# A two-layer decoder trunk on one core: the second product of the feed-forward blocks by Strassen's seven products

## The chip, the cores and the metric

One core of one Trainium2 chip runs the whole program. Time is device microseconds (us) of one execution, taken from three runs without a profile. Beside them one execution was recorded by the hardware profiler. Its span is counted from the first to the last instruction.

The engines named below are PE (matrix products; PEld are its weight loads), DVE (vector), ACT (scalar), POOL (GpSimd), and SP, which issues DMAs. PSUM is the memory in which PE sums products, in eight banks of 128x512 fp32. SBUF is the on-chip memory, HBM the memory outside.

## The reference, cut to what is computed

Two layers, each with four sub-layers (here called phases): `ff1`, a token mixer `mix`, attention into a memory `mem`, and `ff2`. Both feed-forward phases are the same function, so that it runs four times.

```python
D_MODEL, SEQ, DEPTH, D_FF = 1024, 512, 2, 2816
def swiglu(h, w1, w3, w2):
    return (jax.nn.silu(h @ w1) * (h @ w3)) @ w2
for l in range(DEPTH):
    h = rmsnorm(x, ff1_pre_g[l])
    x = x + 0.5 * rmsnorm(swiglu(h, ff1_w1[l], ff1_w3[l], ff1_w2[l]), ff1_post_g[l])
    ... # x = x + rmsnorm(token_mixer(rmsnorm(x))); x = x + rmsnorm(cross_attention(rmsnorm(x), mem))
    h = rmsnorm(x, ff2_pre_g[l])
    x = x + 0.5 * rmsnorm(swiglu(h, ff2_w1[l], ff2_w3[l], ff2_w2[l]), ff2_post_g[l])
```

All is in float32.

## The kernel before

**Products.** A float32 product is made of three products of PE's reduced float32 type: each operand is split into a high part and a remainder, and high by high, high by low and low by high are summed in PSUM (`mm3`, `mm`). Splitting takes ACT for the high part and DVE for the remainder (`split` for activations, `Weights.parts` for weights).

**Weights.** `plan` lists the weight blocks of the whole program in the order of their use. `Weights.pump` issues one SP DMA of 512 KB for each into one of three buffers `raw`. ACT writes the high part and DVE the remainder into one of four buffers `wh`. The remainder frees `raw`; `ahead`, 2 or 4, says how many blocks may be split before their use.

**A feed-forward phase** (`ffn`). The hidden features are 22 blocks of 128. For each, `project` multiplies the normed tokens (`hh`, `hlo`) by a block of w1 and one of w3: 24 matmuls of 128x512 each. `gate` makes the activation from the two banks by a tanh on ACT and two operations on DVE, and splits it into a tile `g`. The first four blocks go through `first_blocks`: all four for tokens 0 to 255 first, then for 256 to 511, so that PE can begin while the last tokens are still normed. This is called the gate stage here.

**The second product** (`token_out`) follows: out = g · w2, by token tiles m = 0 to 3 of 128 tokens, two halves of 512 output features, and 22 blocks of contraction, of which a w2 block holds two. That is 4 x 2 x 22 x 3 = 528 matmuls of 128x512, in four banks for each half of the features. The last four w2 blocks of the second half run token tile by token tile, and after each tile comes its `chain`: a sum of squares on ACT, the product with the gain, small operations on DVE, a power on POOL (`rstd`), and the update of x. Where a phase follows, `pre_norm` norms the token tile, PE transposes it (`tr`), and ACT and DVE split it into `hh` and `hlo`; in the last phase SP writes x to HBM.

**Order.** Each engine runs its instructions in the order in which the program lists them. This order is laid down at build time by a planner (`Clock`), which runs the parts of the code as tasks against estimated times. At run time nothing changes it: an instruction whose input is late holds up all behind it on its engine.

Of the kernel before, what the change touches and what calls it, by code (L numbers as in the profile page):

```python
# [10 lines left out]
F32 = mybir.dt.float32  # L11
F32R = mybir.dt.float32r
# [7 lines left out]
NT = S // 128  # L20
NF = FF // 128
EPS = 1e-6
# [27 lines left out]
def pack(inp):  # L50
# [14 lines left out]
    for f in ("ff1", "ff2"):  # L65
        o[f + "_w1"] = stationary(a[f + "_w1"], NF)
        o[f + "_w3"] = stationary(a[f + "_w3"], NF)
        o[f + "_w2"] = moving(a[f + "_w2"])
# [38 lines left out]

def plan(d):
    items = []

    def add(key, ap, split=True):
        items.append((key, ap, split))

    for l in range(DEPTH):
        for ph in PHASES:
            if ph in ("ff1", "ff2"):
                for i in range(NF):
# [186 lines left out]
class Block:  # L304
    __slots__ = ("raw", "hl", "cols", "ready")


class Weights:


    def __init__(self, b, items, raws, hls):
        self.b, self.items, self.raws, self.hls = b, items, Slots(raws), Slots(hls)
        self.blocks = {}
        self.n_dma = self.n_prep = self.n_use = self.ahead = 0
        self.dma = 0.0

    def pump(self, most=3):
        b, ck = self.b, self.b.ck
        while True:
            moved = False  # L320
            if most and self.n_dma < len(self.items) and self.raws.free:
                most -= 1
                key, ap, split = self.items[self.n_dma]
                k = Block()
                k.cols = ap.shape[-1]
                when, _, k.raw = self.raws.pop()
                k.hl = None
                b.nc.sync.dma_start(k.raw[:, :k.cols], ap)
# [19 lines left out]
    def parts(self, k):  # L348
        b, n = self.b, k.cols
        raw, hi, lo = k.raw[:, :n], k.hl[:, 0, :n], k.hl[:, 1, :n]  # L350
        yield b.act(hi, raw, AF.Copy)
        r = b.tt(lo, raw, hi.bitcast(F32), OP.subtract)
        self.raws.put(r, k.raw)
# [31 lines left out]
class Builder:  # L385
# [70 lines left out]
    def build(self):  # L456
        tc, nc, d, ck = self.tc, self.nc, self.d, self.ck
        with tc.tile_pool(name="fixed", bufs=1) as fixed, \
                tc.tile_pool(name="upper", bufs=1, side="right") as upper, \
                tc.tile_pool(name="small", bufs=4, side="right") as small, \  # L460
                tc.tile_pool(name="psum", bufs=1, space=bass.MemoryType.PSUM) as psum, \
                tc.manual_schedule():
# [4 lines left out]
            raws = [upper.tile([128, 1024], F32, name=f"raw{i}") for i in range(3)]  # L467
# [11 lines left out]
            steps = [(l, ph) for l in range(DEPTH) for ph in PHASES]  # L479
            self.ws = Weights(self, plan(d), raws, wh)  # L480
# [213 lines left out]

    def ffn(self, l, ph):
        tc, nc, ck = self.tc, self.nc, self.ck
        with tc.tile_pool(name=f"{ph}{l}", bufs=1) as pool:
            g = [ck.get(self.hl) for _ in range(12)]
            g += [pool.tile([128, 2, 512], F32R, name=f"g{i}") for i in range(NF - 12)]

            def gate(i, a, b):
                t = yield from ck.take(self.f)
                tv = t[:, :512]
                yield self.act(tv, a, AF.Tanh, scale=0.5)
                self.stt(tv, tv, 1.0, a, OP.add, OP.mult)
                r = self.tt(tv, b, tv, OP.mult)
                self.ps.put(r, a, b)
                yield r
                r = yield from self.split(g[i][:, 0, :], g[i][:, 1, :], tv)
# [864 lines left out]
```

## Time and profile before

| | |
|---|---|
| median of three runs | 2742.8 us (2742.16 to 2742.88) |
| the profiled execution | 2742.21 us |
| its span | 2740.4 us |
| PE busy | 2711.9 us, 99% |
| DVE, ACT, POOL busy | 1422.7, 1039.2, 96.2 us |
| granted PE clock | 0.999 |
| gate stage of one feed-forward phase, about | 239 us |
| its second product, about | 120 us |

The profiled execution lies at the lower end of the three runs and 0.6 us below their median. The page's chain of work that ended last says which engine the end of the program hangs on. The timeline gives start and duration of single instructions, the windows give busy shares of a stretch. PE's matmuls overlap, so the distance between two starts, not the duration printed, is what one matmul costs.

### The profile page before, as it was taken

The page shows a single profiled execution, that of the slowest core. Times are in us where ns is not written, and L with a number is a line of the kernel's source. Part 1 is how long each engine was busy: PE and PEld are TensorE (multiplying, and loading weights), DVE is VectorE, ACT ScalarE, POOL GpSimd, SP SyncE. Part 2 cuts the span into 40 slices and gives each one's busy share as a digit, 9 for nine tenths or more (in the row PEclk, how much of TensorE's full clock was granted, in tenths as well). Part 3 has the DMA queues.
Part 4 walks back from the last instruction along what each step waited for, and adds up shares of the span by engine and source line. Part 5 has one row for each costly group of instructions (what it writes and reads, how often), then busy time and mean ns, then how long its engine had stood idle before and what let it go on. Part 6 is the DMA issues. An engine that isn't in the chain of part 4 may idle for free.

```text
span 2740.4 us, 34447 instructions
## 1 busy us (share of the span) xinstructions
PE 2711.9 (99%) x13628; PEld 2295.3 (84%) x13628; DVE 1422.7 (52%) x2657; ACT 1039.2 (38%) x1896; POOL 96.2 (4%) x179
## 2 busy tenths in 40 slices
PE   8999999999999999999999999999999999999998
PEld 7888888888888888888888888888888798888887
DVE  4443255788646564343353432649886465544323
ACT  4222234455435443222242222445564354422222
POOL 0000010000001000000000000100000010000000
PEclk9999999999999999999999999999999999999999
DMA  4333234312233323332233333342122343233322
GB/s 139 95 112 100 93 96 125 102 60 77 74 111 124 115 77 100 115 100 93 85 100 107 106 95 100 90 136 90 61 70 90 96 150 105 71 100 107 100 94 76
DMA packets 77830, 269.93 MB, mean 98 GB/s; under 512 B 10146, under 2 KB 10658, under 8 KB 77668
## 3 DMA queue, kind: packets, MB, share of 16 engines
q1 hardware_dynamic: 71424, 255.03, 29.1%
q0 software_dynamic: 3136, 10.25, 1.5%
q10 hardware_dynamic: 3108, 2.45, 0.3%
q8 instruction: 106, 1.74, 0.3%
q14 instruction: 56, 0.46, 0.0%
HBM read 265.60 MB, written 2.10 MB: 98 GB/s over the span
## 4 chain that ended last, share of the span: by engine, by line
PE 92%; DVE 4%; ACT 2%; issue 1%; DMA 0%; POOL 0%; ACTq 0%; DVEq 0%; SPq 0%; POOLq 0%
PE ps L414 90%; PE ps L422 3%; ACT junk L393 1%; DVE wh L397 1%; DVE f L397 1%; DVE x L401 0%; DMA x<-in_x_dram 0%; DVE hl L397 0%; ACT wh L393 0%; DVE f L401 0%; DVE f L406 0%; DVE f L1223 0%; DVE mf L397 0%; POOL sty L453 0%; DVE hl L401 0%
## 5 line engine op out<-in xcount | busy, mean ns | idle before, releaser
L414 PE MATMUL ps<-hh,wh 128*128 128x512 f32 (+1 forms) x4864 | 1397.7, 369 | 0.3
L414 PEld LDWEIGHTS ps<-hh,wh 128*128 128x128 f32 x4864 | 881.3, 189 | 148.7 <-issue 1.4
L414 PE MATMUL ps<-hlo,wh 128*128 128x512 f32 (+1 forms) x2432 | 896.8, 369 | 1.8 <-DVE hlo L397 1.8
L397 DVE TENSOR_TENSOR wh<-raw,wh 128x1024 fp32r<-128x1024 f32 x462 | 563.7, 1222 | 642.8 <-ACT wh L393 642.1
L393 ACT ACTIVATE wh<-raw 128x1024 fp32r<-128x1024 f32 x462 | 484.9, 1052 | 706.5 <-PE ps L414 431.1
L414 PEld LDWEIGHTS ps<-hlo,wh 128*128 128x128 f32 x2432 | 459.4, 189 | 76.0 <-DVE hlo L397 2.0
L414 PE MATMUL ps<-wh,hl 128*128 128x512 f32 x2016 | 469.6, 390 | 2.9 <-DVE wh L397 2.9
L414 PEld LDWEIGHTS ps<-wh,hl 128*128 128x128 f32 x2016 | 376.5, 188 | 80.9 <-DVE wh L397 3.7
L397 DVE TENSOR_TENSOR f<-ps,f 128x512 f32<-128x512 f32 (+1 forms) x166 | 114.7, 691 | 289.5 <-PE ps L414 213.0
L414 PE MATMUL ps<-wh,g 128*128 128x512 f32 x960 | 222.2, 390 | 0.0
L414 PEld LDWEIGHTS ps<-wh,g 128*128 128x128 f32 x960 | 179.3, 188 | 36.7
L414 PE MATMUL ps<-hl,wh 128*128 128x512 f32 (+1 forms) x960 | 195.8, 351 | 0.0
L414 PEld LDWEIGHTS ps<-hl,wh 128*128 128x128 f32 x960 | 152.0, 190 | 20.2 <-issue 0.7
L393 ACT ACTIVATE hl<-f 128x512 fp32r<-128x512 f32 (+1 forms) x72 | 45.5, 631 | 241.7 <-DVE f L397 241.7
L393 ACT ACTIVATE hl<-ps 128x512 fp32r<-128x512 f32 (+2 forms) x180 | 81.3, 469 | 118.6 <-PE ps L414 94.9
L397 DVE TENSOR_TENSOR hl<-ps,hl 128x512 fp32r<-128x512 f32 (+2 forms) x180 | 92.1, 529 | 42.6 <-ACT hl L393 42.5
L422 PE MATMUL ps<-ident,f 128*128 128x128 f32 (+1 forms) x582 | 102.2, 279 | 10.6 <-DVE f L401 10.6
L401 DVE SCALAR_TENSOR_TENSOR f<-f,ps 128x512 f32<-128x512 f32 x122 | 83.2, 682 | 53.7 <-PE ps L414 53.6
L393 ACT ACTIVATE g<-f 128x512 fp32r<-128x512 f32 x40 | 25.3, 632 | 181.4 <-DVE f L397 181.4
L422 PEld LDWEIGHTS ps<-ident,f 128*128 128x128 f32 (+1 forms) x582 | 71.4, 140 | 25.8 <-DVE f L401 17.1
L453 POOL TENSOR_TENSOR sty<-v,neghalf 128x1 f32<-128x1 f32 x32 | 23.8, 744 | 1290.4 <-DVE v L408 1272.9
L393 ACT ACTIVATE f<-f,ast 128x32 f32<-128x32 f32 (+4 forms) x120 | 56.0, 468 | 33.1 <-DVE ast L1223 32.4
(185 smaller groups left out, 1868.4 us busy)
## 6 DMA issues: line engine op xcount, KB each, us to landing
raw<-in_ff_w_dram SPq DMA_DIRECT2D x264, 512.0 KB, 3.5
raw<-in_wf_dram SPq DMA_DIRECT2D x80, 512.0 KB, 3.5
raw<-in_cw_dram SPq DMA_DIRECT2D x16, 512.0 KB, 3.6
raw<-in_wmo_dram SPq DMA_DIRECT2D x16, 512.0 KB, 3.7
raw<-in_wq_dram SPq DMA_DIRECT2D x16, 512.0 KB, 3.9
raw<-in_wk_dram SPq DMA_DIRECT2D x16, 512.0 KB, 4.5
raw<-in_wv_dram SPq DMA_DIRECT2D x16, 512.0 KB, 4.0
raw<-in_wo_dram SPq DMA_DIRECT2D x16, 512.0 KB, 3.7
```

Source lines behind the costliest of these rows:

```text
L393: self.nc.scalar.activation(out, src, func, accum_out=accum_out, **kw)
L397: self.nc.vector.tensor_tensor(out, a, b, op)
L401: self.nc.vector.scalar_tensor_tensor(out, a, s, b, op0, op1)
L414: self.nc.tensor.matmul(out, w, x, start=first, stop=last)
L422: self.nc.tensor.transpose(out, src, self.ident)
L453: self.nc.gpsimd.tensor_tensor(out, v[:, :n], self.neghalf[:, :n], OP.pow)
```

## The change

The second product is done in seven products instead of eight (Strassen's scheme). The tokens are halved (A: 256 each), the contraction is paired (an even and an odd block of hidden features: 11 pairs, q = 0 to 10), and the output features are halved (512 each). Each of the seven products has, for each pair, two token tiles of three matmuls of 128x512. That makes 7 x 11 x 2 x 3 = 462 matmuls.

- Products 5, 1 and 4 of a pair run between the gate products (`early`), 18 matmuls for a pair, into six banks of PSUM that stay taken through the gate stage; two banks remain for the gate products. Their weights are a block of 512 columns (`y`) and one of 1024 (`x`), whose halves DVE first adds to and subtracts from each other in `raw` (the operation `combine`).
- Products 3 and 7 (blocks `z1`) and 2 and 6 (`z2`) run after the gate stage. Three of their four weight operands are sums of w2 blocks, which DMAs on POOL's queue form in HBM (`presum`): for each pair two copies (512 KB and 256 KB) and three transfers of 256 KB that add to what is there, 55 DMAs for each feed-forward phase.
- DVE forms the five sums of activation halves and splits seven quarters instead of four (`sides`).
- After the last early product ACT copies the six banks to SBUF (`copies`). DVE combines the copies with the later products: token tiles 0 and 1 after `z1` (`upper`), 2 and 3 after `z2` (`lower`).
- `raw` has four buffers instead of three. w2 takes 3584 columns of weights for each pair where it took 2048. The buffer for POOL's DMA descriptors is set to 8192 bytes.

```diff
 def plan(d):
+    def early(q):
+        add((l, ph, "y", q), pair(w2, l, q, "22"), True, "keep")
+        add((l, ph, "x", q), [(0, pair(w2, l, q, "21")), (HALF, pair(w2, l, q, "11"))], True, "combine")
...
-                for h in range(2):
-                    for i in range(NF // 2):
-                        add((l, ph, "w2", h, i), d[ph + "_w2"][l, h, i])
+                    if i % 2 and 3 <= i < NF - 1:
+                        early(i // 2 - 1)
+                early(NP - 2)
+                early(NP - 1)
+                for q in range(NP):
+                    add((l, ph, "z1", q), z[q, :, :2 * HALF])
+                for q in [NP - 1] + list(range(NP - 1)):
+                    add((l, ph, "z2", q), [(0, pair(w2, l, q, "11")), (HALF, z[q, :, 2 * HALF:])])
     def parts(self, k):
+        if k.op == "combine":
+            one, two = raw[:, :HALF], raw[:, HALF:]
+            b.tt(one, one, two, OP.add)
+            r = b.tt(two, two, k.kept[:, :HALF], OP.subtract)
+            self.raws.put(r, k.kept)
...
         yield b.act(hi, raw, AF.Copy)
         r = b.tt(lo, raw, hi.bitcast(F32), OP.subtract)
-        self.raws.put(r, k.raw)
+        if k.op != "keep":
+            self.raws.put(r, k.raw)
...
-            raws = [upper.tile([128, 1024], F32, name=f"raw{i}") for i in range(3)]
+            raws = [upper.tile([128, 1024], F32, name=f"raw{i}") for i in range(4)]
...
+    def presum(self, l, ph, q):
+        if q < NP:
+            dma(z[q, :, :2 * HALF], w2[l, q, :, HALF:3 * HALF])
+            dma(z[q, :, 2 * HALF:], pair(w2, l, q, "12"))
+        if q > 0:
+            for i, block in enumerate(("22", "22", "11")):
+                dma(z[q - 1, :, i * HALF:(i + 1) * HALF], pair(w2, l, q - 1, block), accum_op=OP.add)
...
     def ffn(self, l, ph):
+            def early(q):
+                y = ws.next((l, ph, "y", q))
+                product(q, 5, y, 0, b5, not q, q == NP - 1)
+                x = ws.next((l, ph, "x", q))
+                product(q, 1, x, HALF, b1, not q, q == NP - 1)
+                product(q, 4, x, 0, b4, not q, q == NP - 1)
...
             for i in range(2, NF):
                 a = self.project((l, ph, "w1", i))
                 b = self.project((l, ph, "w3", i))
+                if i % 2:
+                    self.presum(l, ph, i // 2)
+                    if i < NF - 1:
+                        early(i // 2 - 1)
+            early(NP - 2)
+            early(NP - 1)
...
+            def copies():
+                for b, s in ((b5, s5), (b1, s1), (b4, s4)):
+                    for t in range(2):
+                        k = yield from ck.take(F)
+                        r = self.act(k[:, :512], b[t], AF.Copy)
+                        PS.put(r, b[t])
...
+            def lower(t):
+                m, c21, c22 = 2 + t, s4[t][:, :512], s1[t][:, :512]
+                p = self.tt(c21, b2[t], c21, OP.add)
+                self.tt(c22, c22, b2[t], OP.subtract)
+                q = self.tt(c22, b6[t], c22, OP.add)
...
+            for q in range(NP):
+                blk = ws.next((l, ph, "z1", q))
+                product(q, 3, blk, 0, b3, not q, q == NP - 1)
+                b7 = b7 or [ck.get(PS), ck.get(PS)]
+                product(q, 7, blk, HALF, b7, not q, q == NP - 1)
```

The order of the instructions moves with it at three places.

The first is ACT at the end of the gate stage of the first feed-forward phase (`wh` is a weight block's high part, `g`, `hl` and `hh` those of activations, `f<-ps` a copy or tanh out of a bank). Before:

```order
L393 ACTIVATE g8_147<-f5_96 128x512
L393 ACTIVATE wh1_76<-raw0_72 128x1024
L393 ACTIVATE wh2_77<-raw1_73 128x1024
L393 ACTIVATE wh3_78<-raw2_74 128x1024
L393 ACTIVATE f1_92<-ps4_107 128x512
L393 ACTIVATE g9_148<-f1_92 128x512
L393 ACTIVATE wh0_75<-raw0_72 128x1024
L393 ACTIVATE wh1_76<-raw1_73 128x1024
L393 ACTIVATE wh2_77<-raw2_74 128x1024
```

After:

```order
L426 ACTIVATE wh1_79<-raw1_75 128x1024
L426 ACTIVATE wh2_80<-raw2_76 128x1024
L426 ACTIVATE hh_72<-f0_94 128x256
L426 ACTIVATE wh3_81<-raw3_77 128x1024
L426 ACTIVATE hh_72<-f8_102 128x256
L426 ACTIVATE hh_72<-f7_101 128x512
L426 ACTIVATE wh0_78<-raw0_74 128x1024
L426 ACTIVATE wh1_79<-raw1_75 128x1024
L426 ACTIVATE f3_97<-ps6_112 128x512
L426 ACTIVATE f4_98<-ps1_107 128x512
L426 ACTIVATE f2_96<-ps7_113 128x512
L426 ACTIVATE f6_100<-ps0_106 128x512
```

Before, the last activation's tanh and split stand among blocks of w2. Now the first copy out of the six banks (`f3_97<-ps6_112`) stands behind the high parts of the blocks `z1` 0 to 3; the row `wh1_79<-raw1_75` just ahead of it is the one of `z1` 3, from the buffer that the last `x` block used (first row).

The second is PE where `ff2` of layer 0 meets `ff1` of layer 1, in `first_blocks` (`ps<-ident,f` are transposes of a normed token tile; all others are gate products of one half of the tokens). Before:

```order
L414 MATMUL ps_107<-hh,wh_78 128x256 x2
L414 MATMUL ps_107<-hlo,wh_78 128x256
L414 MATMUL ps_107<-hh,wh_78 128x256 x2
L422 MATMUL ps_106<-ident,f_101 128x128 x4
L414 MATMUL ps_107<-hlo,wh_78 128x256
L414 MATMUL ps_107<-hh,wh_78 128x256 x2
L414 MATMUL ps_107<-hlo,wh_78 128x256
L414 MATMUL ps_107<-hh,wh_78 128x256 x2
L414 MATMUL ps_107<-hlo,wh_78 128x256
L414 MATMUL ps_107<-hh,wh_78 128x256
L422 MATMUL ps_104<-ident,f_96 128x128 x4
L414 MATMUL ps_108<-hh,wh_77 128x256
```

After:

```order
L447 MATMUL ps_113<-hlo,wh_81 128x256
L447 MATMUL ps_113<-hh,wh_81 128x256 x2
L447 MATMUL ps_113<-hlo,wh_81 128x256
L455 MATMUL ps_109<-ident,f_97 128x128 x4
L447 MATMUL ps_113<-hh,wh_81 128x256
L455 MATMUL ps_111<-ident,f_95 128x128 x4
L455 MATMUL ps_106<-ident,f_98 128x128 x4
L455 MATMUL ps_107<-ident,f_104 128x128 x4
L447 MATMUL ps_112<-hh,wh_79 128x256
L447 MATMUL ps_112<-hlo,wh_79 128x256
```

Before, the transposes of token tiles 2 and 3 (four groups) are spread over the last two blocks of the first token half. Now all four stand at the end of that half, and the first product of the other half (`ps_112<-hh,wh_79`) follows.

The third is DVE at the same junction, where the last two token tiles are finished (`sty`, `v`: the small operations of `chain`; `x<-f,sty,x`: the update of x; `wh<-raw,wh`: a weight block's remainder). Before:

```order
L401 SCALAR_TENSOR_TENSOR x<-f_91,sty,x 128x512
L401 SCALAR_TENSOR_TENSOR x<-f_96,sty,x 128x512
L397 TENSOR_TENSOR f_98<-ps_103,f_101 128x512
L397 TENSOR_TENSOR sty<-ssy 128x1
L397 TENSOR_TENSOR wh_75<-raw_74,wh_75 128x1024
L408 TENSOR_SCALAR v<-sty 128x1
L397 TENSOR_TENSOR st<-ssx 128x1
L408 TENSOR_SCALAR v<-st 128x1
L397 TENSOR_TENSOR wh_76<-raw_73,wh_76 128x1024
```

After:

```order
L430 TENSOR_TENSOR sty<-ssy 128x1
L430 TENSOR_TENSOR f_99<-ps_106,f_99 128x512
L430 TENSOR_TENSOR f_96<-f_96,ps_106 128x512
L430 TENSOR_TENSOR f_96<-ps_107,f_96 128x512
L441 TENSOR_SCALAR v<-sty 128x1
L430 TENSOR_TENSOR wh_80<-raw_76,wh_80 128x1024
L430 TENSOR_TENSOR f_99<-f_99,f_102 128x512
L434 SCALAR_TENSOR_TENSOR x<-f_100,sty,x 128x512
L434 SCALAR_TENSOR_TENSOR x<-f_105,sty,x 128x512
L430 TENSOR_TENSOR f_96<-f_96,f_94 128x512
```

Before, the last token tile needs one operation on its bank, the product with the gain (`f_98<-ps_103,f_101`). Now it needs three (`f<-ps,f`, `f<-f,ps`, `f<-ps,f`) and then two products with the gain (`f<-f,f`).

## Rows read from the trace of the kernel before

**Rows 1.** The page: span, busy time of the engines, chain that ended last by engine.
```profile
span 2740.4 us, 34447 instructions
PE 2711.9 (99%) x13628; PEld 2295.3 (84%) x13628; DVE 1422.7 (52%) x2657; ACT 1039.2 (38%) x1896; POOL 96.2 (4%) x179
...
PE 92%; DVE 4%; ACT 2%; issue 1%; DMA 0%; POOL 0%; ACTq 0%; DVEq 0%; SPq 0%; POOLq 0%
```
**Rows 2.** Windows (stretch, length, busy us by engine, clock, DMA share, GB/s): gate stage, second product.
```profile
40.00:240.00 200.00, 200.00 (x903) 166.42 (x902) 84.83 (x96) 59.05 (x77) 2.35 (x4) 1.00 0.33 107
264.00:372.00 108.00, 108.00 (x478) 89.34 (x476) 30.43 (x34) 25.01 (x36) 1.11 (x2) 1.00 0.29 93
```
**Rows 3.** Groups by line, PE, 2613.3 to 2733.2 (last second product): count, busy us, mean ns.
```profile
L414 PE MATMUL ps<-wh,hl 128*128 128x512 f32 x288 | 65.6, 389 | 0.0
L414 PE MATMUL ps<-wh,g 128*128 128x512 f32 x240 | 54.7, 389 | 0.0
```
**Rows 4.** Timeline (start us, length us, operation, count) of PE inside the first second product.
```profile
287.83 7.42 PE L414 MATMUL ps<-wh,hl 128*128 128x512 f32 x32
295.08 5.15 PE L414 MATMUL ps<-wh,g 128*128 128x512 f32 x22
```
**Rows 5.** Timeline of DVE in the gate stage; in brackets idle time before, and its releaser.
```profile
236.35 1.23 DVE L397 TENSOR_TENSOR wh<-raw,wh 128x1024 fp32r<-128x1024 f32 x1 [2.79 <-ACT wh L393]
237.50 0.68 DVE L401 SCALAR_TENSOR_TENSOR f<-f,ps 128x512 f32<-128x512 f32 x1
...
240.88 0.69 DVE L397 TENSOR_TENSOR f<-ps,f 128x512 f32<-128x512 f32 x1 [2.70 <-PE ps L414]
```
**Rows 6.** Timeline of ACT in the same stretch.
```profile
235.26 1.06 ACT L393 ACTIVATE wh<-raw 128x1024 fp32r<-128x1024 f32 x1 [2.95 <-issue]
236.23 0.58 ACT L393 ACTIVATE f<-ps 128x512 f32<-128x512 f32 x1
```
**Rows 7.** DMA, 40 to 240 us: queue (packets, MB, share); issues (KB, us to landing).
```profile
q1 hardware_dynamic: 5555, 20.27, 30.7%
...
raw<-in_ff_w_dram SPq DMA_DIRECT2D x38, 512.0 KB, 3.5
```
**Rows 8.** Timeline of PE where the first `ff1` meets `mix`.
```profile
393.79 0.66 PE L422 MATMUL ps<-ident,f 128*128 128x128 f32 x4 [1.54 <-DVE f L401]
```
**Rows 9.** Timeline of PE where `ff2` of layer 0 meets `ff1` of layer 1.
```profile
1377.45 0.28 PE L414 MATMUL ps<-hh,wh 128*128 128x256 f32 x1
1377.57 0.28 PE L414 MATMUL ps<-hlo,wh 128*128 128x256 f32 x1
...
1389.86 0.60 PE L422 MATMUL ps<-ident,f 128*128 128x128 f32 x4
```
**Rows 10.** Timeline of DVE at the same junction, the operations of token tile 3.
```profile
1379.84 0.68 DVE L397 TENSOR_TENSOR f<-ps,f 128x512 f32<-128x512 f32 x1
...
1387.20 1.41 DVE L401 SCALAR_TENSOR_TENSOR f<-x,st,f 128x512 f32<-128x512 f32 x2
...
1391.12 0.69 DVE L397 TENSOR_TENSOR hlo<-ps,hh 128x512 fp32r<-128x512 f32 x1 [0.70 <-ACT hh L393]
```
**Rows 11.** Timeline of ACT and DVE at the end of the program.
```profile
2733.35 0.60 ACT L393 ACTIVATE junk<-ps 128x512 bf16<-128x512 f32 x1 [4.75 <-PE ps L414]
...
2734.07 0.69 DVE L397 TENSOR_TENSOR f<-ps,f 128x512 f32<-128x512 f32 x1 [2.35 <-ACT junk L393]
...
2735.74 1.41 DVE L401 SCALAR_TENSOR_TENSOR x<-f,sty,x 128x512 f32<-128x512 f32 x2 [0.73 <-POOL sty L453]
```
**Rows 12.** DMA, 390 to 405 us, where POOL's and SP's loads run together.
```profile
q0 software_dynamic: 368, 1.19, 31.2%
q1 hardware_dynamic: 288, 1.05, 21.8%
...
raw<-in_wf_dram SPq DMA_DIRECT2D x1, 512.0 KB, 3.6
...
mf<-in_lng_dram POOLq DMA_DIRECT2D x1, 256.0 KB, 4.9
```

More of the change, by code (lines that the diff above doesn't have):

```diff
@@ L21 @@
 NF = FF // 128
+NP = NF // 2
+HALF = 512
 EPS = 1e-6
@@ L304 @@
 class Block:
-    __slots__ = ("raw", "hl", "cols", "ready")
+    __slots__ = ("raw", "hl", "cols", "ready", "op", "kept")
 class Weights:
@@ L479, in build @@
             steps = [(l, ph) for l in range(DEPTH) for ph in PHASES]
+            d["sums"] = {(l, ph): hbm.tile([NP, 128, 3 * HALF], F32, name=f"z_{ph}{l}") for l, ph in steps
+                         if ph in ("ff1", "ff2")}
             self.ws = Weights(self, plan(d), raws, wh)
@@ L695, in ffn, with gate_a @@
     def ffn(self, l, ph):
-        tc, nc, ck = self.tc, self.nc, self.ck
+        tc, nc, ck, ws, F, H, PS, at = self.tc, self.nc, self.ck, self.ws, self.f, self.hl, self.ps, self.at
         with tc.tile_pool(name=f"{ph}{l}", bufs=1) as pool:
[L698 to L702, printed above, removed]
+            extra = [pool.tile([128, 2, 512], F32R, name=f"g{i}") for i in range(11)]
+            H.put(ck.now, *extra)
+            shared = ck.get(H)
+            quarter = Slots([(shared, 0), (shared, 256)])
+            T, side, held = {}, {}, {}
+            def gate_a(i, a):
+                t = yield from ck.take(F)
@@ L708, in gate @@
                 yield r
[L709 to L718 removed]
+                if i % 2:
+                    yield from sides(i // 2)
@@ new lines, in product @@
+            def product(q, n, blk, c, banks, first, last, ts=(0, 1)):
+                sh, sl = side[q, n]
+                bh, bl = blk.hl[:, 0, c:c + HALF], blk.hl[:, 1, c:c + HALF]
+                for t in ts:
+                    s = slice(t * 128, (t + 1) * 128)
+                    self.mm(banks[t], sh[:, s], bh, first, False)
+                    self.mm(banks[t], sh[:, s], bl, False, False)
+                    self.mm(banks[t], sl[:, s], bh, False, last)
+            b1, b4, b5 = [], [], []
@@ new lines, in ffn @@
+            self.presum(l, ph, NP)
+            early(NP - 2)
+            early(NP - 1)
+            ws.ahead = 4
+            pg = self.load_gain(l, ph, "post")
+            after = self.after
+            norm = self.pre_norms(self.at + 1, self.load_gain(*after, "pre")) if after else None
+            left = [NT]
+            s5, s1, s4, s7 = [], [], [], []
+            def copies():
[4 more added lines that the diff above has]
+                        PS.put(r, b[t])
+                        s.append(k)
+                for t in range(2):
+                    k = yield from ck.take(F)
+                    self.tt(k[:, :512], s1[t][:, :512], s5[t][:, :512], OP.subtract)
+                    s7.append(k)
+                yield r
+                for t in range(2):
+                    k = s7[t][:, :512]
+                    r = self.tt(k, k, s4[t][:, :512], OP.add)
+                ck.signal(("copied", at), r)
@@ L732, in gelu @@
+            for q in range(NP - 1):
+                H.put(ck.now, held[q, 2][1])
+            H.put(ck.now, shared)
+            H.retire(extra)
     def gelu(self, out, z2, zh, t, scale):
```

191 lines of the change are left out of this document (168 added, 23 removed).

## The prediction, on record before the changed kernel ran

> **What bounds the kernel now.** I read the page first: PE is busy 2711.9 of 2740.4 us, and the chain that ended last lies 92% on PE [rows 1]. The windows then show that this holds in both stages of a feed-forward phase: PE is busy all of 200 us and all of 108 us, DVE 42% and 28%, ACT 30% and 23%, and the DMA engines are at 0.33 and 0.29 of their time, all at a granted clock of 1.00, the upper level of 2.4 GHz [rows 2]. So a matmul that is left out is time won, as long as nothing else comes to end last. The groups by line count 288 + 240 = 528 matmuls in one second product [rows 3]. One costs the distance between starts: from 287.83 to 295.08 us stand 32 of them, 0.2266 us each [rows 4]; the mean of 389 ns in [rows 3] is latency.
>
> **The matmuls left out.** 528 - 462 = 66 in each phase, 66 x 0.2266 = 14.96 us, four times 59.8 us. The weight loads go with them one to one. This term can fail only if a matmul got dearer, and its shape stays 128x512.
>
> **What DVE and ACT get more of, in the gate stage.** One pair of hidden blocks takes 4 x 24 = 96 gate matmuls and now 18 early ones: 114 x 0.2266 = 25.8 us. DVE has for it six weight remainders worth 5.5 blocks of 1.23, two times two gate operations of 0.68, the two additions in `raw` of 0.69, and about 2.5 full widths for sums and 3.5 for splits at 0.69 [rows 5]: 6.8 + 2.7 + 1.4 + 4.1 = 15.0, or 58%. ACT has 5.5 x 1.06 and 2 x 0.58 + 3.5 x 0.58 [rows 6]: 9.0, or 35%. Both stay hidden. The two banks left for gate products are tighter: one must be read before the product after the next begins, a block of 24 matmuls (5.44 us) later, while tanh and the two DVE operations need 0.58 + 0.68 + 0.69 = 1.95 us. They can wait behind weights on DVE for some 3 us without loss. I take 0 here, and 1 us for each of nine pairs as the upper bound.
>
> **The end of the gate stage.** Here the order on ACT counts. I count from the end of the last gate product. PE then runs early(9), 18 matmuls, 4.08 us, and product 5 of early(10), to 5.44; 5.67 is when it wants the remainder of the last x block. Queued on DVE ahead of that remainder are the last gate operation (0.6), the y block's remainder (0.6), two half-width sums (0.7), the two additions in `raw` (1.2), and three sums and three splits of half width (2.1); with its own 1.13 it ends at 6.3. (Starts in a row are 0.6 and 1.13 apart; half width is taken at 0.35, an estimate from half of 0.69 [rows 5].) PE waits 0.7. That same remainder frees the buffer for block 3 of z1. Its load takes 3.5 us [rows 7] and lands at 10.0; its high part on ACT (1.06 [rows 6]) stands ahead of the six copies out of the banks, so that the first copy ends at 10.0 + 1.06 + 0.58 = 11.7. PE has ended early(10) at 8.9 and product 3 of the first z1 block at 10.2; product 7 needs a copied bank, and waits 1.5. Together 2.2 us for each phase, 9 in all. Bounds: 0, if the load is issued earlier than I think, and 4, if it takes the 4.9 us of a load that shares the DMA engines with others [rows 12] and the second pair of copies waits too. I keep 2.2, since it is made of rows of this stage.
>
> **z1 and z2.** One block of 512 KB is used for each 12 matmuls, every 2.72 us, where one gate block takes 5.44. That is 193 GB/s, against 107 at a DMA share of 0.33 [rows 2], so a share of 0.6. Four buffers turn over in 3.5 + 1.06 + 1.23 = 5.8 us [rows 5 to 7], or 1.45 us for one, against 2.72. Landing could rise from 3.5 to 8.6 us before PE waits. DVE's 1.13 and ACT's 1.06 in each 2.72 fit. I take 0.
>
> **The sums in HBM.** 55 DMAs on POOL wait for nothing but each other, so they run as a burst from the start of the phase. POOL has the power operations otherwise, 4% of the span [rows 1], and they come before or after. The burst is 8.65 MB of copies and 8.65 MB of additions. In the gate stage 20.27 MB took 0.307 of 200 us of the DMA engines [rows 7], 3.03 us for one MB: 26 us for the copies and 26 f for the additions, if an adding transfer takes f times a plain one. No row shows one. Until the first z1 block, 239 + 45 = 284 us after the phase's start, weights take 31.7 MB, 96 us. The whole fits for 96 + 26 + 26 f < 300, f < 6.8. While POOL's loads took 31.2% of the engines, an SP load landed in 3.6 us [rows 12]; a gate block's load has about 2 x 5.44 - 2.3 = 8.6 us (two blocks ahead, less its splitting). I take 0.
>
> The Trainium skill speaks against this part twice. By "DMA: Bandwidth & Descriptors", section "SWDGE vs HWDGE vs iDMA", DMAs of all issuers run on the same 16 engines and interleave, so the burst takes its time from the weight loads; [rows 12] show both queues sharing. By "Collectives: The Full Stack", section "The bandwidth ceiling: the fold count and why AG ≠ RS ≠ AR", an addition in a DMA needs two source reads and runs at half a copy's rate. With f = 2 the sum above would be 174 of 300 us, and the forecast the same; no row here shows it.
>
> **The junctions.** A phase follows in three of four cases. The last token tile now has three DVE operations at its banks instead of one, but what decides is PE's order: the four transposes of tiles 2 and 3 now stand together behind the first token half. That half takes 96 matmuls of 0.12 us [rows 9], to 11.5 us after the second product's end. The first transposes go at 11.4. On DVE the remainder `hlo` of tile 2 stands ahead of the norm of tile 3 (before, that norm was at 1387.20, 9.75 us after the end [rows 9, 10]). It needs the transposes (0.36) and ACT's split (0.6) and ends near 13.0; the norm takes 1.4, the transposes and the splits of tile 3 follow, and PE's next product has its `hh` and `hlo` at 15.4. Without a wait it would start at 11.5 + 1.44 = 12.96: 2.4 us lost. Before, the first junction with `mix` lost 1.54 [rows 8], and `ff2` to `ff1` nothing (transposes at 1389.86 [rows 9], remainder at 1391.12, beside products [rows 10]). So 2 x 0.9 + 2.4 = 4.2 us. Bounds 0 and 8.
>
> **The tail.** In the last phase the update of x starts at 2735.74, and the second product ended near 2733.1 [rows 11]: 2.6 us. An addition of 0.69 now stands between bank and square, and a product with the gain behind it: 1.5 us more; bounds 0.7 and 2.1, one to three operations of 0.69.
>
> **The sum.** 2742.2 - 59.8 + 9 + 4.2 + 1.5 = 2697.1 us for an execution like the profiled one. The median of the runs lies 0.6 higher: 2698.
>
> **Rivals.**
> 1. *The new waits are hidden.* The load of z1's block 3 goes out earlier, the copies end in time, and transposes wait no more than before: 2698 - 9 - 4.2 - 1.5 = 2683. For it speaks that PE before ran both stages without any gap [rows 2]; against it the order on ACT, which nothing changes at run time.
> 2. *Waits inside the stages.* DVE's order is fixed, and with two banks a gate product waits for DVE where I find slack of some 3 us; 1 us for each of nine pairs is 9 us for a phase, 36 in all: 2734. Or z's loads land later than 8.6 us: at 9.5 us the turn is 11.8 / 4 = 2.95 us instead of 2.72, 22 x 0.23 = 5 us for a phase, 20 in all: 2718. For it: five more DVE operations for each pair depend on each other across engines. Against it: 58% and a share of 0.6.
> 3. *Slower: the sums in HBM come late.* An adding transfer reads and writes the same HBM rows. Above f = 6.8 the last sums end after their use, and each further unit of f costs 26 us for a phase. The gain of 45 is gone at 4 x 26 (f - 6.8) = 45, f = 7.2. At f = 8 it is 2698 + 125 = 2823. For it: no row shows such a transfer, and the chain of five DMAs for each pair is serial in part. Against it: 284 us of cover.
> 4. *The change doesn't do what it says*: the matmuls are fewer, but the freed time fills with waits for weights of 3.5 us in z, where a block is needed every 2.72: 22 x 0.78 = 17 us for a phase, 69 in all: 2767, slower.
>
> **How the numbers follow.** Forecast (stalls as replayed, from half to twice them): 0.52, 2690 to 2712. Rival 1: 0.13. Rival 2: 0.18, 2712 to 2737. Rival 3: 0.11. Rival 4: 0.06. The range goes from rival 1's 2683 to 2730, which leaves out some of rival 2 and rivals 3 and 4. A measurement of this kernel tells 0.2% (5.5 us) from no change. Faster: 0.52 + 0.13 + 0.17 = 0.82; the same, the upper end of rival 2 and the lower of 3 and 4: 0.04; slower 0.14.
>
> **What would show it.** PE's matmuls 264 fewer at 0.2266 us apart. At the end of each gate stage two gaps of PE, about 0.7 (released by DVE's remainder) and 1.5 (by ACT's copy of a bank). In front of the transposes or products of the second token half 2.4 us. No gap of PE released by a weight in z1 or z2, and loads there landing in under 8 us. POOL's DMAs ended long before 284 us of the phase. The forecast is wrong if PE's gaps inside the gate stage sum to more than some us for a phase, or if q0 still runs when z1 begins.

## The result, and the profile after

The changed kernel takes 2703.0 us (median of four runs, 2701.7 to 2705.5), the kernel before 2742.5 beside it: a ratio of 0.9858, 95% interval 0.9846 to 0.987, or 39 us less. The forecast was 2698, the range 2683 to 2730. The profiled execution of the changed kernel is its slowest run, 2705.54 us, against 2742.21 for the one before, 36.7 us less.

The page of the changed kernel, to set against [rows 1]: span, busy time of the engines, POOL's DMA queue (packets, MB, share), the chain that ended last.

```profile
span 2703.8 us, 35696 instructions
PE 2662.2 (98%) x13364; PEld 2251.4 (83%) x13364; DVE 1701.7 (63%) x3293; ACT 1166.4 (43%) x2184; POOL 256.5 (9%) x399
...
q0 software_dynamic: 32000, 79.47, 13.3%
...
PE 92%; DVE 5%; ACT 2%; DMA 1%; issue 1%; POOL 0%; DVEq 0%; SPq 0%; ACTq 0%; POOLq 0%
```

PE has 13628 - 13364 = 264 instructions less, four times 66, and is still what the end hangs on. DVE does 20% more work, and the chain holds little more of it than before, 5% against 4%.

What PE waits for, first in the changed kernel, then in the one before (engine, line and what it waited for: us in total, times, longest).

```profile
PE ps L455 <- DVE f L434: 11.1, 11, 3.9
PE ps L447 <- DVE wh L430: 9.2, 8, 1.4
PE ps L447 <- ACT f L426: 5.9, 4, 2.4
...
PE ps L447 <- DVE hlo L430: 2.8, 4, 1.7
```

```profile
PE ps L422 <- DVE f L401: 10.6, 13, 3.9
PE ps L414 <- DVE wh L397: 5.7, 4, 1.4
...
PE ps L414 <- DVE hlo L397: 1.8, 1, 1.8
```

Two waits are new: 3.5 us for remainders of weights (9.2 - 5.7) and 5.9 us for copies of banks, four of each, one pair for each feed-forward phase. The other two rows grew by 0.5 and 1.0. That is 10.9 us of idle time. 59.8 us of matmuls were left out and 36.7 won, so 23 were lost. The time by phase, read off the timeline of PE in us, shows where:

| from the first gate product to the next phase's first | before | after | difference |
|---|---|---|---|
| `ff1`, layer 0 | 368.79 | 356.18 | -12.61 |
| `mix` and `mem`, layer 0 | 628.35 | 631.12 | +2.77 |
| `ff2`, layer 0 | 364.68 | 351.62 | -13.06 |
| `ff1`, layer 1 | 364.69 | 355.98 | -8.71 |
| `mix` and `mem`, layer 1 | 628.70 | 631.24 | +2.54 |
| `ff2`, layer 1, to the last matmul | 362.02 | 352.46 | -9.56 |
| tail | 7.54 | 9.51 | +1.97 |

A phase's first gate product runs before the last token tiles of the phase ahead are normed, so a junction's waits stand in the phase that follows.

**The end of the gate stage.** PE and ACT wait where the prediction has them wait. The first phase, PE, then ACT (timeline: start, length, operation, count, idle time before and its releaser).

```profile
303.36 1.75 PE L447 MATMUL ps<-wh,hl 128*128 128x512 f32 x7
305.97 4.19 PE L447 MATMUL ps<-wh,hl 128*128 128x512 f32 x17 [0.86 <-DVE wh L430]
311.37 6.91 PE L447 MATMUL ps<-wh,hl 128*128 128x512 f32 x29 [1.21 <-ACT f L426]
```

```profile
309.77 1.06 ACT L426 ACTIVATE wh<-raw 128x1024 fp32r<-128x1024 f32 x1 [1.85 <-DMA raw<-z_ff]
310.74 3.02 ACT L426 ACTIVATE f<-ps 128x512 f32<-128x512 f32 x6
```

PE waits 0.86 us for the remainder of the last x block and 17 matmuls later 1.21 us for a copied bank. ACT meanwhile stands idle for 1.85 us in front of a load from the summed tensor, with the six copies behind it. The idle time printed begins only when the printed duration of the matmul before has run out; by the distance of starts the first wait costs 1.0 us (7 matmuls in 2.61 us, which take 1.59) and the second 1.5 (17 in 5.40, which take 3.85).

**A junction.** PE where `ff2` of layer 0 meets `ff1` of layer 1, to set against [rows 9], and two stretches of it in the windows (stretch, length, busy us of PE, PEld, DVE, ACT, POOL, granted clock, DMA share, GB/s).

```profile
1366.53 0.60 PE L455 MATMUL ps<-ident,f 128*128 128x128 f32 x4
1368.64 1.32 PE L455 MATMUL ps<-ident,f 128*128 128x128 f32 x8 [1.51 <-DVE f L434]
1369.98 0.39 PE L447 MATMUL ps<-hh,wh 128*128 128x256 f32 x1
1370.71 0.39 PE L447 MATMUL ps<-hlo,wh 128*128 128x256 f32 x1 [0.34 <-DVE hlo L430]
...
1372.63 0.63 PE L447 MATMUL ps<-hh,wh 128*128 128x256 f32 x2
1373.06 0.41 PE L447 MATMUL ps<-hlo,wh 128*128 128x256 f32 x1
```

```profile
1371.30:1374.60 3.30, 3.30 (x18) 3.30 (x17) 0.02 (x1) 0.00 (x0) 2.20 (x3) 0.50 0.92 283
1376.00:1386.00 10.00, 10.00 (x77) 9.59 (x76) 6.50 (x9) 4.21 (x8) 4.82 (x8) 1.00 0.98 185
```

The wait was forecast. What follows was not: for 3.3 us the granted clock is 0.50, the lower level of 1.2 GHz, and two matmuls of 128x256 take 0.43 us (1372.63 to 1373.06) where one takes 0.12 at the upper level [rows 9].

### The profile page after: what moved, and what is told of

The parts are those of the page before. It is cut to its first block, busy times and chain, and to the rows that moved or that the text cites. A ratio compares the mean times of both kernels' runs of the same rounds, so it can differ in the third digit from the quotient of the medians.

```text
span 2703.8 us, 35696 instructions
## 1 busy us (share of the span) xinstructions
PE 2662.2 (98%) x13364; PEld 2251.4 (83%) x13364; DVE 1701.7 (63%) x3293; ACT 1166.4 (43%) x2184; POOL 256.5 (9%) x399
## 3 DMA queue, kind: packets, MB, share of 16 engines
q0 software_dynamic: 32000, 79.47, 13.3%
## 4 chain that ended last, share of the span: by engine, by line
PE 92%; DVE 5%; ACT 2%; DMA 1%; issue 1%; POOL 0%; DVEq 0%; SPq 0%; ACTq 0%; POOLq 0%
PE ps L447 89%; PE ps L455 3%; DVE wh L430 1%; ACT junk L426 1%; DVE f L430 1%; DMA raw<-z_ff 1%; ACT wh L426 0%; DVE hl L430 0%; DMA x<-in_x_dram 0%; DVE f L434 0%; DVE x L434 0%; DVE hlo L430 0%; DVE f L439 0%; DVE raw L430 0%; DVE hl L434 0%
## 5 line engine op out<-in xcount | busy, mean ns | idle before, releaser
L430 DVE TENSOR_TENSOR wh<-raw,wh 128x1024 fp32r<-128x1024 f32 (+1 forms) x550 | 641.8, 1175 | 175.6 <-ACT wh L426 174.8
L426 ACT ACTIVATE wh<-raw 128x1024 fp32r<-128x1024 f32 (+1 forms) x550 | 553.8, 1017 | 367.9 <-PE ps L447 209.3
L447 PE MATMUL ps<-wh,hl 128*128 128x512 f32 x1896 | 455.5, 392 | 12.2 <-DVE wh L430 6.3
L447 PEld LDWEIGHTS ps<-wh,hl 128*128 128x128 f32 x1896 | 354.3, 188 | 88.8 <-DVE wh L430 8.9
L426 ACT ACTIVATE f<-ps 128x512 f32<-128x512 f32 (+2 forms) x130 | 71.8, 576 | 481.4 <-PE ps L447 479.9
L447 PE MATMUL ps<-wh,g 128*128 128x512 f32 x720 | 174.6, 390 | 0.0
L447 PEld LDWEIGHTS ps<-wh,g 128*128 128x128 f32 x720 | 134.7, 188 | 27.7
L740 POOL DMA_DIRECT2D z_ff<-in_ff_w_dram x132 | 111.8, 1097 | 167.2 <-DMA z_ff<-in_ff_w_dram 161.4
L426 ACT ACTIVATE hl<-f 128x256 fp32r<-128x256 f32 (+2 forms) x180 | 76.5, 459 | 114.1 <-DVE f L430 114.1
L455 PE MATMUL ps<-ident,f 128*128 128x128 f32 (+1 forms) x582 | 101.6, 279 | 11.1 <-DVE f L434 11.1
L430 DVE TENSOR_TENSOR f<-f,f 128x256 f32<-128x256 f32 (+1 forms) x202 | 98.4, 512 | 14.9 <-ACT f L426 12.4
## 6 DMA issues: line engine op xcount, KB each, us to landing
z_ff<-in_ff_w_dram POOLq DMA_DIRECT2D x44, 512.0 KB, 15.4
```

Of the source, the lines that this page charges most:

```text
L426: self.nc.scalar.activation(out, src, func, accum_out=accum_out, **kw)
L430: self.nc.vector.tensor_tensor(out, a, b, op)
L447: self.nc.tensor.matmul(out, w, x, start=first, stop=last)
L455: self.nc.tensor.transpose(out, src, self.ident)
L740: dma(z[q - 1, :, i * HALF:(i + 1) * HALF], pair(w2, l, q - 1, block), accum_op=OP.add)
```

## Experiments

Times are medians; the changed kernel's 2703.0 is what they are compared with. The kernel before, run beside each of them, had medians of 2741.8 to 2742.5.

**1. Copies ahead of the late block.** Is it the place on ACT that costs the second wait?

```diff
             early(NP - 1)
-            ws.ahead = 4
+            ws.ahead = 2
...
                         PS.put(r, b[t])
                         s.append(k)
+                ws.ahead = 4
+                ws.pump()
```

> Edit: after the last early product only two weight blocks are split ahead instead of four, until the six copies are laid down; so the high part of z1's block 3 stands behind the copies on ACT, and nothing else on ACT moves. Theory (a load at the head of ACT's queue holds up the copies): in the changed kernel ACT waited 1.85 to 3.0 us for that load and PE then 1.2 to 2.4 us for the first copied bank, 6 us in the four phases. Early(10) ends about 1.3 us before product 7 needs its bank, two copies take 1.1: the wait goes to 0 to 0.2, the time falls from 2703 by 5 to 6, to 2697 or 2698. Rival (the late block itself decides, whoever stands behind it): the wait moves to z1's block 3, the time stays at 2703. The wait of about 0.9 for the last x block's remainder stays under both.

Measured: 2693.6 us (2693.0 to 2694.3), ratio 0.9823 (0.9808 to 0.9838). PE, then ACT, at the same place:

```profile
305.56 12.76 PE L447 MATMUL ps<-wh,hl 128*128 128x512 f32 x55 [0.87 <-DVE wh L430]
```

```profile
307.42 3.00 ACT L426 ACTIVATE f<-ps 128x512 f32<-128x512 f32 x6
310.28 2.03 ACT L426 ACTIVATE wh<-raw 128x1024 fp32r<-128x1024 f32 x2
```

55 matmuls run without a gap; the wait for copies is gone from all four phases, and the first wait stands, as expected. The rival falls. The gain is 9.4 us and not 5 to 6. The profiled executions lie 11.9 us apart (2705.5 and 2693.6): 5.9 of it are the idle time for copies. Another 1.4 are low clock that followed the longest of these waits, 2.42 us in the last phase, and 3 are low clock behind the first two junctions, which this execution does not have there; only the third junction has it. So what is more than expected is clock, and since at the junctions this edit gives no reason for that, it is luck in part.

**2. The wait at the junctions filled.** Does the clock fall because PE idled?

```diff
             b = yield from ck.take(self.ps)
+            if h == 0:
+                for _ in range(fill):      # 12 for the last token tile after a feed-forward phase
+                    self.mm(b[:, :256], self.hh[:, 0, :128], self.hh[:, 0, :256], True, True)
             for c in range(4):
                 self.tr(b[:, c * 128:(c + 1) * 128], t[:, c * 128:(c + 1) * 128])
```

> Edit: 12 matmuls of 128x256 whose result nobody reads are put on PE ahead of the transposes of the last token tile, after each feed-forward phase that has a successor; they take 12 x 0.12 = 1.44 us of the 1.51 us in which PE waits there. They go into the bank that the transposes then overwrite. Theory A (the clock falls because PE had idled): in the changed kernel some 16 matmuls behind this wait ran at 0.21 instead of 0.12 us, 1.5 us for each of three junctions; with the wait filled they run at 0.12, and the time falls by 4 to 5 us, to 2698 or 2699, with the same end of DVE's chain. Theory B (the clock falls for another reason, or the matmuls delay the transposes): 2703 or up to 1 us more.

Measured: 2698.5 us (2698.0 to 2699.1), ratio 0.9841 (0.9826 to 0.9856). PE at the junction of layers 0 and 1, and the window behind it:

```profile
1365.16 1.67 PE L447 MATMUL ps<-hh 128*128 128x256 f32 x12
1366.91 1.32 PE L455 MATMUL ps<-ident,f 128*128 128x128 f32 x8
...
1368.98 0.39 PE L447 MATMUL ps<-hlo,wh 128*128 128x256 f32 x1 [0.34 <-DVE hlo L430]
```

```profile
1369.50:1373.50 4.00, 4.00 (x35) 4.00 (x35) 0.58 (x2) 1.54 (x2) 2.84 (x5) 1.00 0.91 247
```

The transposes start no earlier or later after the first half than before (the 1.5 us are filled, not saved), and the clock stays at 1.00 behind all three junctions. 4.5 us less time, and less spread. This bears out theory A: at these places the low clock comes from PE's idle time ahead of it. It does not come every time that PE waits: with the wait unfilled, the profiled executions of the changed kernel and of the other experiments have it at none, one, two or all of the three junctions, at 14 of 30 in ten executions, and the kernel before waited 1.54 us [rows 8] without it. With the wait filled, here and in experiment 7, none of six has it. So the medians, the spread and this count carry the verdict, not one profile. What makes the difference between one unfilled wait and the next is open.

**3. The sums left out, and made two and three times.** What do the DMAs in HBM cost, and from where on?

```diff
-            for i, block in enumerate(("22", "22", "11")):
-                dma(z[q - 1, :, i * HALF:(i + 1) * HALF], pair(w2, l, q - 1, block), accum_op=OP.add)
```

> Edit: the 33 adding DMAs of each feed-forward phase are left out, the copies stay; so the products 2, 3, 6 and 7 get unsummed weights, and the output lacks that part. Theory (the burst is hidden under 284 us of gate stage): the time stays at 2703 within 1 us. The POOL queue's part of the DMA engines' time falls by what the additions took: for f = 2 from about 80 us of 16 engines for a phase to about 27. Rival (weight loads that land at 8.6 us instead of 3.5 during the burst cost PE time somewhere): 2 us less or more than that.

Measured: 2702.8 us (2701.3 to 2703.6), ratio 0.9856 (0.9841 to 0.9871): no difference. First the changed kernel from 20 to 120 us (queue: packets, MB, share; weight loads: KB, us to landing). Then the run without sums: the page's line for POOL's queue over the whole program, and the same window.

```profile
q0 software_dynamic: 6839, 16.64, 75.6%
q1 hardware_dynamic: 3299, 9.64, 27.1%
...
raw<-in_ff_w_dram SPq DMA_DIRECT2D x14, 512.0 KB, 8.6
```

```profile
q0 software_dynamic: 12992, 44.86, 5.6%
...
q0 software_dynamic: 2464, 8.65, 27.4%
...
raw<-in_ff_w_dram SPq DMA_DIRECT2D x14, 512.0 KB, 3.5
```

The burst fills the DMA engines for some 100 us, and weight loads land after 8.6 us instead of 3.5; PE does not wait for them. Copies of 8.65 MB take 27.4 us of the 16 engines; the additions of one phase take (13.3% of 2703.8 - 5.6% of 2701.2) / 4 = 52 us for as much: f = 1.9. "Collectives: The Full Stack" of the Trainium skill, section "The bandwidth ceiling: the fold count and why AG ≠ RS ≠ AR", says of the adding step of a collective that it runs at half the rate of the copying one, because the addition needs two source reads; the ratio in this pair of traces agrees.

Then the whole set of copies and additions once or twice more, into tensors that nobody reads (`sums_twice`, `sums_three`):

```diff
+        for x in self.d["more"][l, ph]:      # one tensor, or two
+            if q < NP:
+                dma(x[q, :, :2 * HALF], w2[l, q, :, HALF:3 * HALF])
+                dma(x[q, :, 2 * HALF:], pair(w2, l, q, "12"))
+            if q > 0:
+                for i, block in enumerate(("22", "22", "11")):
+                    dma(x[q - 1, :, i * HALF:(i + 1) * HALF], pair(w2, l, q - 1, block), accum_op=OP.add)
```

> Edit: each feed-forward phase makes its sums in HBM twice, the second time into a tensor that nobody reads: 110 DMAs on POOL's queue instead of 55, copies and additions both. From the runs so far one set takes 79 us of the 16 DMA engines (27 for the copies, 52 for the additions) and the weight loads a third of their time. Theory (the burst costs nothing until it no longer fits): 158 us at two thirds of the engines is 236 us, before the 284 us at which z1 begins; the time stays at 2703 within 2 us. Rival (each set costs what the saturated engines do to weight loads): 3 us or more slower.

> Edit: the sums are made three times, twice of them into tensors that nobody reads: 165 DMAs for a phase. Theory (capacity): 237 us at two thirds of the engines is 355 us; the sums of the last pairs are ready some 340 us after the phase's start and wanted at 300: 30 to 45 us late in each of four phases, 2820 to 2880, with PE waiting for loads from the summed tensor. Rival (POOL's queue, not the engines' time, paces the sums, or the loads take precedence): under 2750 or above 2950.

Measured: 2701.6 us (2698.6 and 2704.5) twice, 2741.6 (2733.0 to 2743.9) three times, ratios 0.9853 (0.9835 to 0.9871) and 0.9993 (0.9983 to 1.0003). Two sets cost nothing that two runs can show; the third takes the whole gain. The DMA queues of the run with three sets, 20 to 280 us, then its ACT at the end of the gate stage.

```profile
q0 software_dynamic: 18145, 44.39, 74.8%
q1 hardware_dynamic: 9452, 27.25, 29.6%
...
raw<-in_ff_w_dram SPq DMA_DIRECT2D x38, 512.0 KB, 9.4
```

```profile
310.11 1.06 ACT L426 ACTIVATE wh<-raw 128x1024 fp32r<-128x1024 f32 x1 [3.22 <-DMA raw<-z_ff]
313.23 1.06 ACT L426 ACTIVATE wh<-raw 128x1024 fp32r<-128x1024 f32 x1 [2.07 <-DMA raw<-z_ff]
314.20 3.02 ACT L426 ACTIVATE f<-ps 128x512 f32<-128x512 f32 x6
```

The border lies where capacity puts it, between two sets and three, but the price expected of the third, 117 to 177 us, was three to nearly five times the measured 38.6. POOL's queue held three quarters of the engines' time and not two thirds: 3 x 79 / 0.75 = 316 us instead of 355, and the last of its DMAs was in fact issued at 319, the last that belongs to the sums in use at 307. Even then weight loads landed after 9.4 us and PE ran the gate stage without a gap. The loss begins at its end, where the burst still runs: SP's loads of z1 land after 8.9 us (4.7 in the changed kernel, both from 300 to 335 us), and SP waited six times for a sum, 25.3 us in all. PE's idle time for copies grew from 5.9 to 22.9 us, for remainders from 9.2 to 14.9, in front of transposes from 11.1 to 16.7; that is 28 of the 38. The granted clock was at 0.50 for 34 us ahead of the tail instead of 13.6, which makes the other 10, an estimate at half of the difference.

**4. The last x block earlier.** Does the first wait hang on DVE's order?

```diff
+            ws.ahead = 3
             early(NP - 2)
             early(NP - 1)
             ws.ahead = 4
```

> Edit: three weight blocks instead of two are split ahead of their use from the last but one early pair on, nothing else. The addition, subtraction and remainder of the last x block then stand on DVE ahead of the last pair's splits. Theory (both waits at the end of the gate stage hang on that remainder): product 1 no longer waits 0.9; instead product 5 waits some 0.4 for its activations, which now stand behind; the buffer for z1's block 3 comes free 2 us earlier, it lands 2 us earlier, and the first copied bank is there in time: 0.4 lost instead of 2.1 in each phase, and in the last one 3 instead of 0.4: 2703 - 8 = 2695, with one low-clock stretch less now and then. Rival (DVE only changes the order in which things come late): 2701 to 2705.

Measured: 2696.7 us (2694.8 to 2697.0), ratio 0.9832 (0.9818 to 0.9845). The wait for remainders is back at 5.7 us in all, the wait for copies is 1.3; in their place product 5 waits 0.7 for its activations, 3.0 in all. The theory holds in kind, and the rival falls; the replacing wait was 0.7 and not 0.4.

**5. Three buffers.**

```diff
-            raws = [upper.tile([128, 1024], F32, name=f"raw{i}") for i in range(4)]
+            raws = [upper.tile([128, 1024], F32, name=f"raw{i}") for i in range(3)]
```

> Edit: three weight buffers instead of four in the changed kernel. Theory (a buffer turns over in 3.5 to 4.5 us of landing and 2.3 of splitting, 6.8 us or 2.3 for one of three, against 2.72 for a block of z): z loses nothing; the end of the gate stage loses up to 2 us more for each phase, since the y block and the x block hold two buffers there: 2703 to 2711. Rival (loads that land at 8.6 us in the burst and the kept y block leave too few buffers): PE waits inside the gate stage, 10 us or more for a phase, 2743 or more.

Measured: 2702.2 us (2700.4 to 2703.8), ratio 0.9855 (0.9841 to 0.9868). The fourth buffer brings nothing that can be measured, and the loss of up to 2 us expected at the end of each gate stage did not come. No wait for weights appears in z1 or z2, as the prediction's term of 0 has it.

**6. What decides at the junctions.** Three edits take work from DVE there. First the order in the tail:

```diff
                     product(q, 2, blks[n], 0, b2, False, n == 3, (t,))
+                ck.spawn(lower(t), ck.now + ck.LAT)
+                for n, q in enumerate(order[-4:]):
                     product(q, 6, blks[n], HALF, b6, False, n == 3, (t,))
...
-                ck.spawn(lower(t), ck.now + ck.LAT)
+                ck.signal(("b6", at, t), ck.now + ck.LAT)
```

> Edit: in the tail of the second product, for each token tile the products 2 of the last four blocks come first and then the products 6 (before: block by block), and the first two DVE operations of a tile start after the products 2. Of the last tile, one addition instead of two additions, a subtraction and a product with the gain is left behind the last matmul. Theory A (the last tile's chain decides at junctions and tail): x is updated 1.2 to 1.8 us earlier in the tail, and each of the three junctions loses 1 to 1.5 us less: 2697 to 2699. Theory B (at the junctions the DVE's whole queue decides: the remainder of tile 2 stands ahead of the norm of tile 3, and four weight remainders among them): the tail gains 1.2 to 1.8 and the junctions 0 to 0.4: 2701.

Measured: 2703.8 us (2703.5 to 2705.0), ratio 0.986 (0.9844 to 0.9876). That is above both theories. The tail is 0.8 us shorter (8.70), but PE's wait in front of the last transposes grew from 1.5 to 1.85 us at all three junctions.

Then the product with the gain of token tiles 2 and 3 on POOL, and left out:

```diff
-                return self.tt(y, y, pg[h][:, :512], OP.mult)
+                if m < 2:
+                    return self.tt(y, y, pg[h][:, :512], OP.mult)
+                nc.gpsimd.tensor_tensor(y, y, pg[h][:, :512], OP.mult)
+                return ck.op("g", 1.2)
```

> Edit: the product with the gain of token tiles 2 and 3 (four of 128x512 in each feed-forward phase) runs on POOL instead of DVE. Theory (at the junctions the work queued on DVE decides: from the end of the second product to the last remainder 14 us of it stand there): four operations of 0.6 less, of which two or three stood behind the end: 1.2 to 1.8 us less wait at each of three junctions, 2698 to 2700. Rival (POOL takes 2 us or more for one, and the update of x waits for it): the junctions lose as much or more, the tail 1 to 3 us more: 2703 to 2712.

> Edit: the product with the gain of token tiles 2 and 3 is left out (four DVE operations of 128x512 in each feed-forward phase), so that the output lacks this factor. Theory A (at the junctions the work queued on DVE decides): 1.2 to 1.8 us less wait at each of three junctions and 0.6 to 1.2 in the tail: 2697 to 2699. Theory B (the place of the transposes behind the first token half on PE decides, and DVE waits for them): 0.5 or less at a junction: 2701 to 2702.

Measured: 2705.4 us (2704.2 to 2706.1) on POOL, ratio 0.9866 (0.9853 to 0.988); 2699.2 (2698.7 to 2701.5) left out, ratio 0.9846 (0.9832 to 0.9859). On POOL it is the rival's time, though not by the rival's reason: one product took POOL 1.3 to 1.7 us and not 2 or more. Left out, the time is close to theory A's 2697 to 2699, but the traces do not show its mechanism. The tail gains 1.1 us, and `ff1` of layer 1 2.35, of which 1.5 is a low-clock stretch that this execution does not have; so this junction gains 1 us at most for the four operations. At the two junctions with `mix` nothing is gained: the wait of 1.5 us comes there as two, 0.75 and 0.9. The rest of the gain is one more low-clock stretch that did not come. DVE of that run at the junction of the layers (its first gate product is at 1355.25, 1354.58 in the changed kernel), and behind it DVE of the changed kernel:

```profile
1366.18 0.69 DVE L430 TENSOR_TENSOR hlo<-ps,hh 128x512 fp32r<-128x512 f32 x1 [0.54 <-ACT hh L426]
...
1367.87 1.41 DVE L434 SCALAR_TENSOR_TENSOR f<-x,st,f 128x512 f32<-128x512 f32 x2 [0.73 <-POOL st L486]
1370.00 1.36 DVE L430 TENSOR_TENSOR hlo<-ps,hh 128x512 fp32r<-128x512 f32 x2 [0.71 <-ACT hh L426]
```

```profile
1367.24 0.69 DVE L430 TENSOR_TENSOR hlo<-ps,hh 128x512 fp32r<-128x512 f32 x1 [1.58 <-ACT hh L426]
1367.85 1.40 DVE L434 SCALAR_TENSOR_TENSOR f<-x,st,f 128x512 f32<-128x512 f32 x2
```

In the changed kernel DVE idles for 1.58 us in front of the remainder of tile 2, which waits for the row transposes and ACT's split, and the norm of tile 3 stands behind it. So its wait hangs on this chain and not on DVE's load: theory B of the run with the product left out, and of the run with the other order only that the remainder stands ahead of the norm. With less work on DVE the planner laid down another order, in which DVE still idles between the two, for POOL's power. An order of the changed kernel in which only tile 3's norm is put ahead of tile 2's remainder was not tried.

**7. All three edits that helped.** Experiments 1 and 2, and of 4 a closer form: three blocks ahead only until the y block of the last but one pair is taken.

```diff
                 y = ws.next((l, ph, "y", q))
+                ws.ahead = 2
...
+            ws.ahead = 3
             early(NP - 2)
             early(NP - 1)
-            ws.ahead = 4
+            ws.ahead = 2
```

> Edit: copies first, as before; the last x block alone is split one block earlier (three blocks ahead only until the last but one pair's y block is taken, then two), so that its remainder stands on DVE ahead of the last pair's splits but no block of z1 does; and 12 matmuls fill the wait in front of the last tile's transposes at the three junctions. Theory (the three losses are separate and add up): the wait of 0.9 for the remainder goes in all four phases (3.5), the wait for the copies as in the run with copies first, and no junction has a low-clock stretch: 2693.6 - 3.5 - 1 = 2688 to 2690. Rival (the last pair's activations or z1's first block are late in its place, as 0.5 to 0.7 us of waiting for activations in the run with the earlier x block): 2691 to 2693.

Measured: 2688.3 us (2687.6 to 2688.5), ratio 0.9804 (0.9791 to 0.9818), 14.7 us less than the changed kernel. PE at the end of the first gate stage:

```profile
301.61 1.52 PE L447 MATMUL ps<-wh,g 128*128 128x512 f32 x6
302.97 9.23 PE L447 MATMUL ps<-wh,hl 128*128 128x512 f32 x40
```

No gap is left there, nor in the other three phases, and no low clock ahead of the tail. The time is that of the theory, in which the three losses add up. It is the fastest of all kernels run here.

## Why the prediction was right, point by point

- **The matmuls left out** (59.8 us): right. 264 fewer, and the median distance of two 128x512 matmuls is 0.227 us in both traces.
- **DVE and ACT in the gate stage, two banks, the burst** (0): right. PE has no gap in any of the four gate stages before their last pair, though DVE's share rose from 42% to 55% of such a stage (139.73 of 253 us from 27 to 280 us).
- **End of the gate stage** (0.7 and 1.5 in each phase, 9 in all): 0.87 and 1.1 to 1.2 us of idle time in the first three phases, 0.87 and 2.4 in the last, 9.4 in all. By the distance of starts, as the prediction counts, it is 2.5 to 2.6 in each of the first three and 3.8 in the last, 11.5 in all; the last phase lost 1.4 more to low clock. Experiments 1, 4 and 7 show both causes as the prediction named them: the place of the remainder on DVE, and that of z1's block 3 on ACT.
- **z1 and z2** (0): right; experiment 5.
- **The sums** (0, with f below 6.8): right. f is 1.9, and the border lies between two and three sets of 79 us. Rival 3 names a real border. In its terms three sets are f = 8.1 (26 + 26 f = 237 us); for f = 8 it has 125 us, and 38.6 were measured (experiment 3).
- **The junctions** (4.2): the wait was right, 1.5 + 0.34 us idle and 15.4 us from the second product's end to the first product of the second token half (1354.58 to 1369.98). The cost was mis-sized. The two phases `mix` with `mem` lost 5.3 us, and `ff1` of layer 1 gained 4.1 us less than the mean of the other two of layer 0: 9.4 in all. 4.5 of it are low-clock matmuls behind the waits, which the prediction did not have: it took what PE runs after a wait at the distance of [rows 9]. The other 0.7 beyond the forecast 4.2 is not followed up.
- **The tail** (1.5): 1.97 us.
- **The sum.** 2697.1 was forecast for an execution like the profiled one, 2705.5 came, 8.4 more. 4.5 us of low clock and 0.7 of other cost more than forecast at the junctions, 2.5 at the ends of the gate stages, 1.4 of low clock in the last phase and 0.5 in the tail make 9.6. Three waits of 0.22, 0.35 and 0.35 us inside second products of the kernel before are gone, 0.9 that the prediction did not count. The changed kernel's four runs spread from 2701.7 to 2705.5; with no low clock at the junctions it takes 2698.5 (experiment 2). So the forecast of 2698 had the waits about right and missed the clock behind them. Of the rivals none is needed.

## What to carry to other kernels

When PE is busy all the time, matmuls that are left out are won less what is lost where a long stage hands over: of 59.8 us this kernel won 39.5 at first, and 54 with the three edits at those places. Look there in each engine's order for an instruction that waits for a load ahead of others that free a bank or a buffer. A wait of PE of under 2 us cost up to 1.6 us more here, in low clock behind it; 12 matmuls whose result nobody reads, put in its place, cost nothing. Transfers that nothing paces were hidden up to the capacity of the DMA engines, and doubling and tripling them shows how far that is.

## What the hardware showed that was not expected

- After waits of PE of 1.5 and 0.34 us in a row the granted clock fell to 0.50 for some 3 us, 1.4 to 1.6 us lost each time, but only at 14 of the 30 junctions. Waits for copies of 2.4 to 2.6 us in four executions were followed by it, one of 2.67 in another was not.
- While POOL multiplied a 128x512 tile, DVE took 1.9 us for a weight remainder that takes 1.22. POOL, then DVE, in the run with the gain on POOL:

```profile
1357.02 1.30 POOL L897 TENSOR_TENSOR f<-f,f 128x512 f32<-128x512 f32 x1 [2.65 <-ACT junk L426]
1358.28 1.53 POOL L486 TENSOR_TENSOR sty<-v,neghalf 128x1 f32<-128x1 f32 x1
```

```profile
1357.49 1.91 DVE L430 TENSOR_TENSOR wh<-raw,wh 128x1024 fp32r<-128x1024 f32 x1
```

"SBUF — State Buffer" of the Trainium skill, section "Who interferes with whom", says that a DVE instruction with two SBUF inputs contends with a GpSimd instruction that reads SBUF; the trace agrees, 0.7 us for one of them. In that run PE waits 0.85 and 0.73 us for a weight remainder at the junctions with `mix`, which the changed kernel does not, and the tail is 0.9 us longer, where POOL's 1.3 us stand in the place of DVE's 0.7. That this is all that kept the edit from gaining is not shown.
